# The memory norm's factors in two lots, and the decode output of attention two tiles earlier

## The chip, the cores and the metric

One core of one Trainium2 chip runs one launch of the program. The metric is the device time of the launch in microseconds (us), the median of several runs. The names of the engines: PE is the matrix engine (TensorE), DVE VectorE, ACT ScalarE, POOL GpSimd, SP SyncE, whose work here is to issue DMAs; each takes its instructions in an order fixed when the program is built.

## The reference

One step of a decoder layer over a prompt of 1024 tokens and a sample group of 8 sequences with one new token each. Only the part around the change is given:

```python
xp = xp + merge_groups(oa, o_r, gr, subln_a[l], lam_init).astype(xp.dtype) @ w_out[l]
mk_p, mv_p = mem_kv(mem_prompt, norm_mem_kv[l], w_mk[l], w_mv[l])
xp = xp + mem_attend(rmsnorm(xp, norm_mem_q[l]), mk_p, mv_p, w_mq[l], w_mo[l])
xp = xp + sq_relu_mlp(rmsnorm(xp, norm_mlp[l]), w_up[l], w_down[l])

def rmsnorm(x, g):
    xf = x.astype(jnp.float32)
    y = xf * lax.rsqrt(jnp.mean(xf * xf, axis=-1, keepdims=True) + EPS)
    return (y * g.astype(jnp.float32)).astype(x.dtype)

def mem_attend(h, mk, mv, w_mq, w_mo):
    q = (h @ w_mq).reshape(B, T, H_M, DH_M)
    s = jnp.einsum('bthd,bmhd->bhtm', q, mk.astype(q.dtype)).astype(jnp.float32) * DH_M ** -0.5
    p = jax.nn.softmax(s, axis=-1)
    ...
```

The sample group goes through the same lines with the same weights; its attention reads caches of keys and values by pages. All is float32 and the model width is 1024.

## The kernel before

The 1024 prompt tokens and the 8 decode tokens stand side by side as T = 1032 columns, cut into three thirds of CH = 344; c = 2 is the third (columns 688 to 1031), which holds the decode tokens. Activations lie with the features on the partitions, eight feature tiles of 128. Each operand of a product is split into a high and a low part (UH and UL, wh and wl), so that one product of 8 feature tiles is 24 matmuls.

A weight unit u (512 KB) is loaded by SP into `raw_u`, cast to `wh_u` by ACT and subtracted to `wl_u` by DVE. `raw` has three buffers, `wh` and `wl` four. The query weights of memory attention are u48 to u55, two units for each of four pairs of feature tiles.

`proj_residual` multiplies attention's output by `w_out` and adds the residual. Its tiles `pr_o_ft_c` go in the order (0,0), (0,1), (1,0) ... (7,1), and then the late third (0,2) ... (7,2). The first five of the late third are begun with half of their terms behind (7,1) and finished later, because the decode columns of the other half are not there yet. Behind each tile DVE adds the residual into `x2_ft` (L1447), ACT squares it, and POOL adds the square to `ssum2` (L1497). The finished `x2` is stored to DRAM as X2 (L1587), and it is split with the norm's gain into UH and UL: 688 columns early, the late third at the end.

Beside these tiles the steps of `decode_values` run: attention of the decode tokens over cached values. They sum into `dacc` on DVE; then `dop` (two matmuls) sums over partitions, `oda` (ACT, DVE and POOL) normalises the heads, and `dtr` (four transposes) brings the result into the decode columns of UH and UL. A list of tiles, `when`, says behind which tile a step goes.

`rstd_bcast` makes the norm's factors: matmuls with a vector of ones sum the squares over the features into `rs`; ACT copies the sums into a row; SP moves that row into 86 partitions (`rcol`); DVE and POOL take the power -0.5; SP stores the factors to DRAM (`rrow`, row 2) and reads them back into all partitions as `rb2`. The query product `mq_pr_f_c` does not need the factors; they multiply its result (L1679, into `qm`), for which six PSUM banks are there.

From the decode columns of `qm` POOL makes `qdm`, DVE `dex_m`, and PE `rep_m_0`, a transposed copy of the decode queries, which stands behind the second pair's two late products. In the same stretch the memory's keys and values are prepared: `memT` (split to `mh` and `ml`) and `memn` (squared, `mjk`), whose own factors `rm` are stored to DRAM in single floats (L1629) and read back as `rmb` (L1631).

The code is written in program order, and a scheduler merges it into one order for each engine and for SP's queue. `pin` holds PE's matmuls to the written order.

Of the kernel before, what the change touches and what calls it, by code (L numbers as in the profile page):

```python
# [19 lines left out]
P = 128  # L20
D = 1024
# [27 lines left out]
def decoder_step(ctx: ExitStack, tc: tile.TileContext, i: dict, o: dict):  # L49
# [24 lines left out]
    def mm(out, l, r, start, stop):  # L74
        pinned(nc.tensor.matmul(out, l, r, start=start, stop=stop))  # L75
# [4 lines left out]
    def mm3(out, terms, lo=0, hi=None):  # L80
        n = len(terms)
        for x, (lh, ll, rh, rl) in list(enumerate(terms))[lo:hi]:
            mm(out, lh, rh, x == 0, False)
            mm(out, lh, rl, False, False)
            mm(out, ll, rh, False, x == n - 1)
# [51 lines left out]
    def rsqrt_small(out, ss, n, scale, p=P):  # L137

        nc.vector.tensor_scalar(ss, ss, scale, EPS, ALU.mult, ALU.add)
        nc.gpsimd.tensor_tensor(out, ss, half[:p, 0:1].to_broadcast([p, n]), op=ALU.pow)  # L140
# [28 lines left out]
    def bcast_rows(row_ap, p, n):  # L169
        return bass.AP(tensor=row_ap.tensor, offset=row_ap.offset, ap=[[0, p], [1, n]])  # L170
# [1253 lines left out]
            pass  # L1424


    def proj_residual(A, bank, base, ktorder, xsrc, xdst, ssum, nm, us0, steps, when, parts, ahead=0, early=None, stage=()):

        squares = []
        units = {p: us0[2 * p : 2 * p + 2] for p in range(len(us0) // 2)}

        def fetch(p):
            if p not in units:
                units[p] = [unit(base + 2 * p + x, parts(2 * p + x) if p > 1 else None, nc.gpsimd if p == 1 else None) for x in range(2)]
            for ft in (2 * p, 2 * p + 1):
                nc.sync.dma_start(xdst(ft), xsrc(ft))

        def terms(ft, c):
            return proj_terms(units[ft // 2], ft % 2, c, ktorder)

        def store(ps, ft, c):
            cs = slice(c * CH, c * CH + CH)
            xd = xdst(ft)[:, cs]
            nc.vector.tensor_add(xd, ps[:, :CH], xd)  # L1447
            seen["DVE"] = nc.cur_bb.bb.instructions[-1]
            if (ft, c) == (7, 2):
                last = A.tile([P, WMAX], F32, tag="sqc", name=f"sqc_{nm}_7_2", bufs=2)[:, :CH]  # L1450
                nc.scalar.activation(last, xd, AF.Square)
                squares.append(last)
            else:
                add_squares(A, xd, ssum, cs, ft == 0, f"{nm}_{ft}_{c}")


        order = [(ft, c) for ft in range(8) for c in range(2)] + [(ft, 2) for ft in range(8)]
        fetch(0)
        fetch(1)
        early = early or {}  # L1460
        pin[0] = ahead > 0
        for ft, c in order[:ahead]:
            if (ft, c) not in early:
                early[ft, c] = bank(f"pr_{nm}_{ft}_{c}"), 0
            ps, done = early[ft, c]
            mm3(ps[:, :CH], terms(ft, c), done, 7)
            early[ft, c] = ps, 7
        for ft, c in order:
            if (ft, c) in ((1, 1), (2, 1)):
                fetch(ft + 1)  # L1470
            if (ft, c) in early:
                ps, done = early[ft, c]
                mm3(ps[:, :CH], terms(ft, c), done)
            else:
                pin[0] = False
                ps = bank(f"pr_{nm}_{ft}_{c}")
                mm3(ps[:, :CH], terms(ft, c))
            seen["PE"] = nc.cur_bb.bb.instructions[-1]
            store(ps, ft, c)
            if (ft, c) in when:  # L1480
                next(steps)
            if (ft, c) == (7, 1):
                for some in stage:
                    for x in some:
                        early[x] = bank(f"pr_{nm}_{x[0]}_{x[1]}"), 4
                        mm3(early[x][0][:, :CH], terms(*x), 0, 4)
                    seen["PE"] = nc.cur_bb.bb.instructions[-1]
                    next(steps)
        return squares[0]

    def add_squares(A, x, ssum, cs, first, nm):
        if first:
            nc.scalar.activation(ssum[:, cs], x, AF.Square)
        else:
            sq = A.tile([P, WMAX], F32, tag="sqc", name=f"sqc_{nm}", bufs=2)[:, : cs.stop - cs.start]
            nc.scalar.activation(sq, x, AF.Square)
            nc.gpsimd.tensor_add(ssum[:, cs], ssum[:, cs], sq)  # L1497

    def rstd_bcast(A, PS, bufs, ssum, last, r, dst, nm, rtag):

        row = A.tile([P, T], F32, tag=rtag, name=f"rrow_{nm}")[:1]
        rp = PS.tile([P, 512], F32, tag="acc", name=f"rs_{nm}", bufs=bufs)
        sums = [rp[32 * c : 32 * c + 1, :CH] for c in range(3)]
        for c in range(3):
            mm(sums[c], ones, ssum[:, c * CH : c * CH + CH], True, c < 2)
        mm(sums[2], ones, last, False, True)
        for c in range(3):
            nc.scalar.copy(row[:, c * CH : c * CH + CH], sums[c])
        col = A.tile([86, 12], F32, tag="rcol", name=f"rcol_{nm}")
        nc.sync.dma_start(col, row)  # L1510
        rc = A.tile([86, 12], F32, tag="rrc", name=f"rrc_{nm}")
        rsqrt_small(rc, col, 12, 1.0 / D, 86)
        nc.sync.dma_start(rrow[r : r + 1, :].rearrange("a (p c) -> p (a c)", p=86), rc)
        nc.sync.dma_start(dst, bcast_rows(rrow[r : r + 1, :], P, T))

    with pool("x2") as XP:
        x2 = [XP.tile([P, T], F32, tag=f"x2_{ft}", name=f"x2_{ft}") for ft in range(8)]
# [2 lines left out]
        with pool("c") as A:  # L1520
            def decode_values():
# [26 lines left out]
                with tc.issue_after(seen["PE"]):  # L1548
# [12 lines left out]
                    odv = oda.rearrange("p (h v) -> p h v", h=4)  # L1561
                    nc.vector.tensor_mul(odv, odv, r4.unsqueeze(2).to_broadcast([8, 4, P]))
                yield
                with tc.issue_after(seen["PE"]):
                    tr = dt("dtr")
                    for h in range(4):
                        nc.tensor.transpose(tr[:, h * 8 : h * 8 + 8], oda[:, h * P : h * P + P], ident[:8, :8])
                    odT = tr[:, :32].rearrange("p (k c) -> p k c", k=4)
                    for h in range(4):
                        split_gain(odT[:, h, :], subln8, h, NT, T, gcol=0)  # L1570
                yield


            ssum = A.tile([P, T], F32, tag="ssum", name="ssum2")
            last = proj_residual(
                A, out_bank, U_OUT, OUT_KT, lambda ft: i["xT"][:, ft, :], lambda ft: x2[ft], ssum, "o", us_out, decode_values(),
                [(ft, c) for ft in range(4) for c in range(2)] + [(4, 1)],
                lambda x: [
                    G.tile([P, T], F32R, tag="rb2", name="wlo_3")[:, :1024] if (nm, x) == ("wl", 7)
                    else A.tile([P, 1024], F32R, tag=f"{nm}{x}", name=f"{nm}o_{x}") for nm in ("wh", "wl")  # L1580
                ],
                ahead=len(OUT_EARLY), early=early_out, stage=([(0, 2), (1, 2)], [(2, 2), (3, 2), (4, 2)]),
            )
            rb2 = G.tile([P, T], F32, tag="rb2", name="rb2")
            rstd_bcast(A, PB, 2, ssum, last, 2, rb2, "2", "dacc")
            for ft in range(8):
                nc.sync.dma_start(X2[ft], x2[ft])  # L1587
        bc_ps.close()
# [7 lines left out]
    with pool("d") as A:  # L1596
# [62 lines left out]
        for pr in range(4):  # L1659
            us = [unit(U_MQ + 2 * pr + x) for x in range(2)]  # L1660
            for f in range(2):
                qm.append(A.tile([P, T], F32, tag=f"qm{2 * pr + f}", name=f"qm_{2 * pr + f}"))

            late = [(0, 2), (1, 2)]
            rest = [(0, 0), (0, 1), (1, 0), (1, 1)]
            for f, c in late + rest if pr else rest + late:
                q = qm[2 * pr + f]
                cs = slice(c * CH, c * CH + CH)
                ps = PS.tile([P, 512], F32, tag="acc", name=f"mq_{pr}_{f}_{c}", bufs=6)
                mm3(  # L1670
                    ps[:, :CH],
                    [
                        (us[kt // 4][0][:, (kt % 4) * 256 + f * P : (kt % 4) * 256 + f * P + P],
                         us[kt // 4][1][:, (kt % 4) * 256 + f * P : (kt % 4) * 256 + f * P + P],
                         UH[:, kt, cs], UL[:, kt, cs])
                        for kt in range(8)
                    ],
                )
                nc.vector.scalar_tensor_tensor(q[:, cs], ps[:, :CH], -1.0 / 16.0, rb2[:, cs], ALU.mult, ALU.mult)  # L1679
                if c == 2:  # L1680
                    nc.gpsimd.tensor_copy(qdm[:, 2 * pr + f, :], q[:, NT:])
                if (f, c) == (1, 2) and pr % 2:
                    for _ in dec:
                        pass
                    dec = dec_scores(pr // 2)
                    next(dec)
                for _ in range(3 if pr == 3 else 1):
                    next(dec, None)
# [938 lines left out]
```

## Time and profile before

| | |
|---|---|
| median of 3 runs | 1488.96 us (1487.69 to 1489.63) |
| the profiled execution's own time | 1496.69 us |
| its span, first to last instruction | 1494.8 us |
| mean granted clock of PE | 0.995 |
| PE busy | 1471.7 us, 98% of the span |
| DVE, ACT, POOL busy | 73%, 45%, 21% |
| mean DMA rate | 158 GB/s |

The profile is one execution; times in it are counted from its first instruction, and L with a number is a line of the kernel before. Buffer numbers are left out of the names there, so `pr_o` stands for all its tiles and `rb` for `rb2`. A number behind `<-` in brackets is the idle time of the engine before an instruction, and the name there what ended it.

### The profile page before, as it was taken

The numbers are of one execution on the slowest core, as the hardware profiler recorded it, in microseconds if no ns is written. First come the engines' busy times: TensorE is split into PE (matmuls) and PEld (weight loads), VectorE is DVE, ScalarE is ACT, GpSimd is POOL, SyncE is SP. The second block draws the span as 40 slices with busy tenths as digits, with TensorE's granted clock in tenths as the row PEclk, the third lists the DMA queues.
The fourth block names the chain that finished last, engine by engine and source line by source line (L and its number), as shares of the span: only waits on it lengthen the run. The fifth ranks groups of instructions, "written<-read, shape, count | busy, mean of one in ns | idle before, by whom it ended". The sixth has DMA issues, their size and how long they took to land.

```text
span 1494.8 us, 27880 instructions
## 1 busy us (share of the span) xinstructions
PE 1471.7 (98%) x10925; PEld 1401.8 (94%) x10925; DVE 1098.7 (73%) x2264; ACT 679.6 (45%) x1325; POOL 321.1 (21%) x346
## 2 busy tenths in 40 slices
PE   9999999998999999999999999999999999999997
PEld 7899779998779999989999999999999999999997
DVE  7666436887767636567886988888888879787865
ACT  7543435665552431248535643434334443343454
POOL 0035323123414311105022100000001311110380
PEclk9999999999999999999999999999999999999998
DMA  8255728213847157474582444344436774536273
GB/s 287 65 185 180 202 58 189 71 47 110 268 145 283 59 195 175 145 228 102 178 304 68 136 148 145 128 154 157 156 139 209 239 251 142 171 101 198 72 128 114
DMA packets 125238, 236.69 MB, mean 158 GB/s; under 512 B 13748, under 2 KB 76521, under 8 KB 124978
## 3 DMA queue, kind: packets, MB, share of 16 engines
q1 hardware_dynamic: 89064, 170.51, 36.0%
q0 software_dynamic: 24912, 44.80, 11.0%
q10 hardware_dynamic: 11130, 19.60, 3.5%
q8 instruction: 86, 1.41, 0.4%
q14 instruction: 46, 0.38, 0.1%
HBM read 170.25 MB, written 57.52 MB: 152 GB/s over the span
## 4 chain that ended last, share of the span: by engine, by line
PE 84%; DVE 8%; ACT 3%; issue 2%; DMA 2%; POOL 0%; ACTq 0%; another core or an unknown queue 0%; SPq 0%; DVEq 0%; POOLq 0%
PE dn L2309 19%; PE Z L2143 9%; PE qkp L75 7%; PE mq L75 6%; PE Y L2143 6%; PE X L2143 6%; PE pr_o L75 6%; PE pr_m L75 4%; PE grp L75 3%; PE sp L75 2%; PE av L75 2%; PE mv L75 1%; PE mk L75 1%; PE mpv L75 1%; PE vap_z L522 1%
## 5 line engine op out<-in xcount | busy, mean ns | idle before, releaser
L2309 PE MATMUL dn<-UH,wd 128*128 128x258 f32 x1792 | 325.1, 283 | 0.8 <-DVE c L2413 0.3
L2309 PEld LDWEIGHTS dn<-UH,wd 128*128 128x128 f32 x1792 | 277.6, 189 | 1.8 <-issue 0.8
L2309 PE MATMUL dn<-UL,wd 128*128 128x258 f32 x896 | 252.7, 282 | 0.0
L2309 PEld LDWEIGHTS dn<-UL,wd 128*128 128x128 f32 x896 | 169.0, 189 | 0.0
L2413 DVE TENSOR_TENSOR c<-c,dn 128x258 f32<-128x258 f32 x216 | 88.5, 417 | 38.2 <-PE dn L2309 35.8
L2169 ACT ACTIVATE hq<-r 128x258 f32<-128x258 f32 x128 | 53.9, 422 | 114.1 <-DVE r L2168 114.1
L2143 PE MATMUL X<-UH,wu 128*128 128x258 f32 x512 | 97.4, 282 | 0.9 <-ACT p L2194 0.9
L2143 PE MATMUL Z<-T_h,wu 128*128 128x258 f32 x512 | 98.2, 284 | 0.0
L2287 ACT CAST wd<-raw_d 128x512 fp32r<-128x512 f32 x96 | 58.8, 620 | 78.4 <-PE dn L2309 73.2
L1953 ACT CAST wu<-raw_up 128x512 fp32r<-128x512 f32 x96 | 59.2, 617 | 62.2 <-PE Z L2143 54.7
L2280 ACT CAST UH<-raw_h 128x1032 fp32r<-128x1032 f32 x56 | 58.8, 1057 | 55.0 <-PE dn L2309 27.3
L2143 PEld LDWEIGHTS X<-UH,wu 128*128 128x128 f32 x512 | 81.3, 188 | 1.1 <-ACT p L2194 1.1
L2143 PEld LDWEIGHTS Z<-T_h,wu 128*128 128x128 f32 x512 | 81.3, 189 | 0.0
L2281 DVE TENSOR_TENSOR UL<-raw_h,UH 128x1032 fp32r<-128x1032 f32 x56 | 73.4, 1311 | 9.9 <-ACT UH L2280 9.9
L2180 POOL DMA_DIRECT2D HT<-ht x32 | 17.2, 536 | 292.4 <-DVE ht L2179 291.9
L2288 DVE TENSOR_TENSOR wd<-raw_d,wd 128x512 fp32r<-128x512 f32 x96 | 72.0, 757 | 10.0 <-ACT wd L2287 9.9
L2143 PE MATMUL Z<-T_l,wu 128*128 128x258 f32 x256 | 72.3, 282 | 0.0
L2143 PE MATMUL X<-UL,wu 128*128 128x258 f32 x256 | 72.3, 282 | 0.0
L128 ACT CAST wh_u<-raw_u 128x1024 fp32r<-128x1024 f32 x43 | 44.7, 1049 | 54.2 <-PE mq L75 31.2
L1954 DVE TENSOR_TENSOR wu<-raw_up,wu 128x512 fp32r<-128x512 f32 x96 | 64.5, 684 | 3.7 <-ACT wu L1953 3.7
L129 DVE TENSOR_TENSOR wl_u<-raw_u,wh_u 128x1024 fp32r<-128x1024 f32 x39 | 51.6, 1328 | 18.3 <-ACT wh_u L128 18.1
L2301 POOL TENSOR_TENSOR raw_d<-raw_d,raw_d 128x512 f32<-128x512 f32 x16 | 22.1, 1382 | 194.5 <-DVE raw_d L2297 173.4
(598 smaller groups left out, 4718.2 us busy)
## 6 DMA issues: line engine op xcount, KB each, us to landing
raw_u<-in_wall SPq DMA_DIRECT2D x49, 512.0 KB
HT<-ht POOLq DMA_DIRECT2D x32, 516.0 KB
raw_h<-HT SPq DMA_DIRECT2D x32, 516.0 KB
raw_up<-in_wall SPq DMA_DIRECT2D x32, 512.0 KB
raw_d<-in_wall SPq DMA_DIRECT2D x32, 512.0 KB
HQ<-hq ACTq DMA_DIRECT2D x32, 387.0 KB
raw_h<-HQ SPq DMA_DIRECT2D x24, 516.0 KB
cmk<-in_cmk SPq DMA_DIRECT2D x16, 512.0 KB
```

Of the source, the lines that this page charges most:

```text
L75: pinned(nc.tensor.matmul(out, l, r, start=start, stop=stop))
L129: (lo_engine or nc.vector).tensor_sub(wl[:, :n], raw[:, :n], wh[:, :n].bitcast(F32))
L1953: nc.scalar.copy(w[:, :512], src)
L1954: nc.vector.tensor_sub(w[:, 512:], src, w[:, :512].bitcast(F32))
L2143: pinned(nc.tensor.matmul(ps, l, r[:, k, :], start=first and k == 0 and x == 0, stop=k == 3 and x == 2, skip_group_check=True))
L2169: nc.scalar.activation(h[:, PLACE[quad], :], r, AF.Square)
L2280: nc.scalar.copy(h, rv)
L2281: nc.vector.tensor_sub(l, rv, h.bitcast(F32))
L2287: nc.scalar.copy(w[:, :512], src)
L2288: nc.vector.tensor_sub(w[:, 512:], src, w[:, :512].bitcast(F32))
L2309: pinned(nc.tensor.matmul(ps, l, r[:, k, cq], start=first and k == 0 and x == 0, stop=k == 3 and x == 2, skip_group_check=True))
L2413: nc.vector.tensor_add(y, y, ps)
```

## The change

It has two parts.

The decode output: `dop` and `oda` go behind tile (6,1); `dtr` stays where it was (an empty step stands between).

The factors: the squares of the late third go into a tile of their own, `third` (`ssum3_o`), which takes one of the three `raw` buffers. The sums of the first two thirds of the columns (`rs_2`) are formed behind tile (4,2), and their factors (8 in each of 86 partitions) go the old way into columns 0 to 687 of `rb2`. The late third's sums (`rs_3`, two matmuls) stand behind the first query product, mq_0_0_0, and their factors (4 in each of 86 partitions) go into the rest of `rb2` by DMAs of their own.

```diff
@@ -1424,12 +1424,12 @@
             pass
 
 
-    def proj_residual(A, bank, base, ktorder, xsrc, xdst, ssum, nm, us0, steps, when, parts, ahead=0, early=None, stage=()):
-        squares = []
+    def proj_residual(A, bank, base, ktorder, xsrc, xdst, ssum, nm, us0, steps, when, parts, sums_done, ahead=0, early=None, stage=()):
+        third = []
         units = {p: us0[2 * p : 2 * p + 2] for p in range(len(us0) // 2)}
 
         def fetch(p):
@@ -1446,10 +1446,13 @@
             xd = xdst(ft)[:, cs]
             nc.vector.tensor_add(xd, ps[:, :CH], xd)
             seen["DVE"] = nc.cur_bb.bb.instructions[-1]
-            if (ft, c) == (7, 2):
-                last = A.tile([P, WMAX], F32, tag="sqc", name=f"sqc_{nm}_7_2", bufs=2)[:, :CH]
-                nc.scalar.activation(last, xd, AF.Square)
-                squares.append(last)
+            if c == 2:
+                if ft == 0:
+                    third.append(G.tile([P, T], F32, tag="raw", name=f"ssum3_{nm}", bufs=3))
+                if ft == 7:
+                    nc.scalar.activation(third[0][:, CH : 2 * CH], xd, AF.Square)
+                else:
+                    add_squares(A, xd, third[0], slice(0, CH), ft == 0, f"{nm}_{ft}_{c}")
             else:
                 add_squares(A, xd, ssum, cs, ft == 0, f"{nm}_{ft}_{c}")
 
@@ -1479,6 +1482,8 @@
             store(ps, ft, c)
             if (ft, c) in when:
                 next(steps)
+            if (ft, c) == (4, 2):
+                sums_done()
             if (ft, c) == (7, 1):
                 for some in stage:
                     for x in some:
@@ -1486,7 +1491,7 @@
                         mm3(early[x][0][:, :CH], terms(*x), 0, 4)
                     seen["PE"] = nc.cur_bb.bb.instructions[-1]
                     next(steps)
-        return squares[0]
+        return third[0]
 
     def add_squares(A, x, ssum, cs, first, nm):
         if first:
@@ -1496,22 +1501,21 @@
             nc.scalar.activation(sq, x, AF.Square)
             nc.gpsimd.tensor_add(ssum[:, cs], ssum[:, cs], sq)
 
-    def rstd_bcast(A, PS, bufs, ssum, last, r, dst, nm, rtag):
-        row = A.tile([P, T], F32, tag=rtag, name=f"rrow_{nm}")[:1]
-        rp = PS.tile([P, 512], F32, tag="acc", name=f"rs_{nm}", bufs=bufs)
-        sums = [rp[32 * c : 32 * c + 1, :CH] for c in range(3)]
-        for c in range(3):
-            mm(sums[c], ones, ssum[:, c * CH : c * CH + CH], True, c < 2)
-        mm(sums[2], ones, last, False, True)
-        for c in range(3):
+    def token_rstd(cols, row, sums, terms, r, cs, nm):
+        n = (cs.stop - cs.start) // 86
+        for c in range(n // 4):
+            for x, y in enumerate(terms):
+                mm(sums[c], ones, y[:, c * CH : c * CH + CH], x == 0, x == len(terms) - 1)
+        for c in range(n // 4):
             nc.scalar.copy(row[:, c * CH : c * CH + CH], sums[c])
-        col = A.tile([86, 12], F32, tag="rcol", name=f"rcol_{nm}")
-        nc.sync.dma_start(col, row)
-        rc = A.tile([86, 12], F32, tag="rrc", name=f"rrc_{nm}")
-        rsqrt_small(rc, col, 12, 1.0 / D, 86)
-        nc.sync.dma_start(rrow[r : r + 1, :].rearrange("a (p c) -> p (a c)", p=86), rc)
-        nc.sync.dma_start(dst, bcast_rows(rrow[r : r + 1, :], P, T))
+        col, rc = cols[:, 0:n], cols[:, n : 2 * n]
+        nc.sync.dma_start(col, row[:, : n * 86])
+        rsqrt_small(rc, col, n, 1.0 / D, 86)
+        nc.sync.dma_start(rrow[r : r + 1, cs].rearrange("a (p c) -> p (a c)", p=86), rc)
+    def spread_rstd(dst, r, cs):
+        nc.sync.dma_start(dst[:, cs], bcast_rows(rrow[r : r + 1, cs], P, cs.stop - cs.start))
 
     with pool("x2") as XP:
         x2 = [XP.tile([P, T], F32, tag=f"x2_{ft}", name=f"x2_{ft}") for ft in range(8)]
@@ -1561,6 +1565,7 @@
                     odv = oda.rearrange("p (h v) -> p h v", h=4)
                     nc.vector.tensor_mul(odv, odv, r4.unsqueeze(2).to_broadcast([8, 4, P]))
                 yield
+                yield
                 with tc.issue_after(seen["PE"]):
                     tr = dt("dtr")
                     for h in range(4):
@@ -1572,17 +1577,25 @@
 
 
             ssum = A.tile([P, T], F32, tag="ssum", name="ssum2")
-            last = proj_residual(
+            early_tokens, late_tokens = slice(0, 2 * CH), slice(2 * CH, T)
+            def first_rstd():
+                rp = PB.tile([P, 512], F32, tag="acc", name="rs_2", bufs=2)
+                row = A.tile([P, T], F32, tag="dacc", name="rrow_2")[:1]
+                cols = A.tile([86, 16], F32, tag="rcol", name="rcol_2")
+                token_rstd(cols, row, [rp[32 * c : 32 * c + 1, :CH] for c in range(2)], [ssum], 2, early_tokens, "2")
+            third = proj_residual(
                 A, out_bank, U_OUT, OUT_KT, lambda ft: i["xT"][:, ft, :], lambda ft: x2[ft], ssum, "o", us_out, decode_values(),
-                [(ft, c) for ft in range(4) for c in range(2)] + [(4, 1)],
+                [(ft, c) for ft in range(4) for c in range(2)] + [(4, 1), (6, 1)],
                 lambda x: [
                     G.tile([P, T], F32R, tag="rb2", name="wlo_3")[:, :1024] if (nm, x) == ("wl", 7)
                     else A.tile([P, 1024], F32R, tag=f"{nm}{x}", name=f"{nm}o_{x}") for nm in ("wh", "wl")
                 ],
-                ahead=len(OUT_EARLY), early=early_out, stage=([(0, 2), (1, 2)], [(2, 2), (3, 2), (4, 2)]),
+                first_rstd, ahead=len(OUT_EARLY), early=early_out, stage=([(0, 2), (1, 2)], [(2, 2), (3, 2), (4, 2)]),
             )
             rb2 = G.tile([P, T], F32, tag="rb2", name="rb2")
-            rstd_bcast(A, PB, 2, ssum, last, 2, rb2, "2", "dacc")
+            spread_rstd(rb2, 2, early_tokens)
             for ft in range(8):
                 nc.sync.dma_start(X2[ft], x2[ft])
         bc_ps.close()
@@ -1667,6 +1680,7 @@
                 q = qm[2 * pr + f]
                 cs = slice(c * CH, c * CH + CH)
                 ps = PS.tile([P, 512], F32, tag="acc", name=f"mq_{pr}_{f}_{c}", bufs=6)
+                pin[0] = (pr, f, c) == (0, 0, 0)
                 mm3(
                     ps[:, :CH],
                     [
@@ -1676,6 +1690,12 @@
                         for kt in range(8)
                     ],
                 )
+                if pin[0]:
+                    token_rstd(
+                        third[:86, 2 * CH : 2 * CH + 8], A.tile([P, T], F32, tag="qm7", name="rrow_3")[:1], [dt("rs_3")[:1, :CH]],
+                        [third[:, :CH], third[:, CH : 2 * CH]], 2, late_tokens, "3")
+                    spread_rstd(rb2, 2, late_tokens)
+                    pin[0] = False
                 nc.vector.scalar_tensor_tensor(q[:, cs], ps[:, :CH], -1.0 / 16.0, rb2[:, cs], ALU.mult, ALU.mult)
                 if c == 2:
                     nc.gpsimd.tensor_copy(qdm[:, 2 * pr + f, :], q[:, NT:])
```

In the scheduled orders more moves than these lines. On PE before, all sums stand ahead of the query product (`rs_2` of the three thirds; `sqc_o_7_2` is the last square):

```order
L75 MATMUL pr_o_7_2_5602<-UL_67,who_7_5057 128x344
L75 MATMUL pr_o_7_2_5602<-UH_66,wlo_3_5058 128x344
L75 MATMUL rs_2_5632<-ssum2_4950,ones_62 1x344 x3
L75 MATMUL rs_2_5632<-sqc_o_7_2_5628,ones_62 1x344
L75 MATMUL mq_0_0_0_5757<-UH_66,wh_u48_5745 128x344
L75 MATMUL mq_0_0_0_5757<-UL_67,wh_u48_5745 128x344
```

On PE now, first behind pr_o_4_2 and then behind mq_0_0_0:

```order
L75 MATMUL pr_o_4_2_5440<-UH_66,wlo_5_5010 128x344
L75 MATMUL rs_2_5545<-ssum2_4950,ones_62 1x344 x2
L75 MATMUL pr_o_5_2_5556<-UH_66,who_4_5003 128x344
...
L75 MATMUL mq_0_0_0_5753<-UH_66,wl_u49_5748 128x344
L75 MATMUL rs_3_5779<-ssum3_o_5479,ones_62 1x344 x2
L75 MATMUL mq_0_0_1_5789<-UH_66,wh_u48_5741 128x344
```

The sums went from ahead of the query product to these two places.

SP's queue before, from the factors' row on (`rcol_2`, `rrow` and `rb2` are the norm's factors; `rm` is the store of the memory factors):

```order
L1510 DMA rcol_2_5640<-rrow_2_5631 86x1x12
L1513 DMA rrow_75<-rrc_2_5642 86x12
L1514 DMA rb2_5630<-rrow_75 128x1032
L1606 DMA g_mkv_5699<-in_g_mkv 128x8
L1613 DMA memT_0_5705<-in_memT 128x1024
L1613 DMA memT_1_5715<-in_memT 128x1024
L1624 DMA memn_0_5726<-in_mem 128x1024
L1624 DMA memn_1_5730<-in_mem 128x1024
L1643 DMA cmk_0_0_5997<-in_cmk 128x2x512
L1643 DMA cmk_0_2_6029<-in_cmk 128x2x512
L1629 DMA rrow_75<-rm_5734 128x2x1
L1643 DMA cmk_0_4_6061<-in_cmk 128x2x512
```

SP's queue now, first from the store of X2 to the early factors and then the part with the late ones (`ssum3_o` is now also the place of the late factors' 86 partitions):

```order
L1600 DMA X2_71<-x2_4_4941 128x1032
L1513 DMA rcol_2_5547<-rrow_2_5546 86x1x8
L122 DMA raw_u49_5745<-in_wall 128x1024
L1600 DMA X2_71<-x2_5_4942 128x1032
L1515 DMA rrow_75<-rcol_2_5547 86x8
L122 DMA raw_u50_5921<-in_wall 128x1024
L1600 DMA X2_71<-x2_6_4943 128x1032
L122 DMA raw_u51_5927<-in_wall 128x1024
L1518 DMA rb2_5641<-rrow_75 128x688
L1600 DMA X2_71<-x2_7_4944 128x1032
L122 DMA raw_u52_6131<-in_wall 128x1024
L122 DMA raw_u53_6137<-in_wall 128x1024
```

```order
L1619 DMA g_mkv_5695<-in_g_mkv 128x8
L1626 DMA memT_0_5701<-in_memT 128x1024
L1626 DMA memT_1_5711<-in_memT 128x1024
L1637 DMA memn_0_5722<-in_mem 128x1024
L1513 DMA ssum3_o_5479<-rrow_3_5778 86x1x4
L1637 DMA memn_1_5726<-in_mem 128x1024
L1656 DMA cmk_0_0_6003<-in_cmk 128x2x512
L1515 DMA rrow_75<-ssum3_o_5479 86x4
L1656 DMA cmk_0_2_6035<-in_cmk 128x2x512
L1642 DMA rrow_75<-rm_5730 128x2x1
L1518 DMA rb2_5641<-rrow_75 128x344
L1656 DMA cmk_0_4_6067<-in_cmk 128x2x512
```

The loads of u48 to u52, which stood ahead of all stores of X2 before, now stand among them; u53 and u52 stand ahead of `memT`; the late factors' row, second last of these rows, stands behind the store of `rm`.

ACT before, around the last square of the late third:

```order
L144 ACTIVATE UH_66<-x2_2_4939,g_mq_4945 128x344
L144 ACTIVATE UH_66<-x2_3_4940,g_mq_4945 128x344
L1451 ACTIVATE sqc_o_7_2_5628<-x2_7_4944 128x344
L144 ACTIVATE UH_66<-x2_7_4944,g_mq_4945 128x344
L1508 COPY rrow_2_5631<-rs_2_5632 1x344 x3
```

ACT now, at the same place:

```order
L144 ACTIVATE UH_66<-x2_3_4940,g_mq_4945 128x344
L128 CAST wh_u50_5923<-raw_u50_5921 128x1024
L1453 ACTIVATE ssum3_o_5479<-x2_7_4944 128x344
L144 ACTIVATE UH_66<-x2_7_4944,g_mq_4945 128x344
L128 CAST wh_u51_5929<-raw_u51_5927 128x1024
L1511 COPY rrow_3_5778<-rs_3_5779 1x344
```

The casts of u50 and u51 went in between the late splits and the square.

## The prediction

> **What bounds the kernel now.** I read the busy shares first, then the chain that ended last.
>
> ```profile
> PE 1471.7 (98%) x10925; PEld 1401.8 (94%) x10925; DVE 1098.7 (73%) x2264; ACT 679.6 (45%) x1325; POOL 321.1 (21%) x346
> PE 84%; DVE 8%; ACT 3%; issue 2%; DMA 2%; POOL 0%; ACTq 0%; another core or an unknown queue 0%; SPq 0%; DVEq 0%; POOLq 0%
> ```
>
> PE is the bound from end to end, so a term counts only if it takes PE time away or leaves PE waiting. In the stretch that the change touches (495 to 640 us) the waits of PE are two:
>
> ```profile
> PE dtr L1567 <- DVE oda L1562: 1.0, 1, 1.0
> PE rs L75 <- ACT sqc_o L1451: 1.0, 1, 1.0
> ```
>
> The timeline of PE shows both places (columns: start, duration, instruction, idle before), and the chain that ended last, in order of time, what comes after:
>
> ```profile
> 505.93 1.03 PE L75 MATMUL dop<-dacc,selgt 128*8 128x512 f32 x4
> ...
> 512.50 0.32 PE L75 MATMUL pr_o<-UH,wlo 128*128 128x344 f32 x1
> 513.82 0.38 PE L1567 MATMUL dtr<-ident,oda 8*128 8x8 f32 x4 [1.00 <-DVE oda L1562]
> ...
> 535.02 0.32 PE L75 MATMUL pr_o<-UH,wlo 128*128 128x344 f32 x1
> 535.27 0.75 PE L75 MATMUL rs<-ssum,ones 128*1 128x344 f32 x6
> 537.01 0.74 PE L75 MATMUL rs<-sqc_o,ones 128*1 128x344 f32 x2 [0.98 <-ACT sqc_o L1451]
> 537.68 0.42 PE L75 MATMUL mq<-UH,wh_u 128*128 128x344 f32 x1
> ```
>
> ```profile
> 512.99 0.69 DVE oda L1562
> ...
> 537.75 30.34 PE mq L75 x192
> 568.08 0.22 PE rep_m L854 x2
> ...
> 569.31 0.22 PE rep_m L854
> ```
>
> A matmul of 344 columns takes PE 30.34 / 192 = 0.158 us in the stream.
>
> The sums of squares keep PE from the query product from 535.18 (535.02 + 0.16) to 537.68: 2.5 us, of which 0.98 is waiting. The factors that follow from them bind nothing in this trace: no PE wait follows. All my terms are differences; they are made against this execution's 1494.8 us span (its own time was 1496.69, the median of the runs 1488.96), and I carry them to the median one for one.
>
> **The decode output two tiles earlier.** `dop` moves from behind three half groups to ahead of pr_o_7_0; its two matmuls cost the same there. The sums that it needs are old by then. Everything between `dop` and the transposes took 7.8 us before (505.93 to 512.99 + 0.69) and now has the two tiles and five half groups, 108 matmuls by 0.158 = 17 us. So the wait of 1.0 goes. The `oda` steps now stand on DVE ahead of the sum of pr_o_7_0 and hold it up by a few us; the banks are seven and the next user of that bank is seven groups on, so this costs nothing. Taken: -1.0; bounds -1.1 and -0.8.
>
> **The sums in two lots.** The three first matmuls of `rs` ran side by side in 0.75 (six passes, 535.27). Two of them move behind pr_o_4_2, where `ssum` has long been summed: +0.8 there. The third lot is two matmuls into one row, one after the other: a single one took 537.68-537.01 = 0.67, so 1.3, behind the first query product. Against 2.5 before this is -0.4.
>
> ```profile
> 529.08 0.92 POOL L1497 TENSOR_TENSOR ssum<-ssum,sqc_o 128x344 f32<-128x344 f32 x1 [2.18 <-ACT sqc_o L1496]
> 541.46 2.28 POOL L140 TENSOR_TENSOR rrc<-rcol,half 86x12 f32<-86x12 f32 x1 [7.35 <-DVE rcol L139]
> ...
> 532.94 3.03 ACT L144 ACTIVATE UH<-x,g_mq 128x344 fp32r<-128x344 f32 x6
> 536.46 0.49 ACT L1451 ACTIVATE sqc_o<-x 128x344 f32<-128x344 f32 x1 [0.49 <-DVE x L1447]
> ```
>
> It presumes that the last square is there when PE has done mq_0_0_0, 24 matmuls or 3.8 us after the last pr_o. With both terms the last pr_o ends at 535.0 (535.18-1.0+0.8), so the square is due at 538.8. ACT now casts wh_u50 right ahead of it, and raw_u50 is loaded only behind the first factors on SP's queue: pr_o_5_2 ends 48 matmuls before 535.0, at 527.4; its sum and square (0.5 each), POOL's addition (0.9) and POOL's power (8 columns, so 1.6 of the 2.28 for 12) bring that to 531, and the load to 531.5. A load of that size with nothing in front took 3.6 us (`memn`, below): landed at 535.1. ACT's splits end at 536.0, then the cast (about 1.0) and the square (0.5): 537.5. This hides, with 1.3 us to spare; bounds 0 and +1.5, as far as the stores in front may hold the load.
>
> **The queues that it is moved past.** On SP the loads of u48 to u53 now stand between and behind the X2 stores, and the row of the late factors stands behind `memT` and `memn`. On DVE the subtractions wl_u49 to wl_u51, done by 524.8 before, fall among the last splits:
>
> ```profile
> 523.59 1.23 DVE L129 TENSOR_TENSOR wl_u<-raw_u,wh_u 128x1024 fp32r<-128x1024 f32 x1 [0.41 <-ACT wh_u L128]
> ...
> 535.87 0.50 DVE L1447 TENSOR_TENSOR x<-pr_o,x 128x344 f32<-128x344 f32 x1
> 536.29 1.74 DVE L145 SCALAR_TENSOR_TENSOR UL<-x,g_mq,UH 128x344 fp32r<-128x344 f32 x3
> ```
>
> The splits ended at 538.0; with two and a half such subtractions (1.2 each) wl_u51 ends near 541. raw_u53 waits for it, because it gets raw_u51's buffer, and `g_mkv` and `memT` stand behind it. What follows `memT` then goes as it did, only earlier:
>
> ```profile
> 545.47 0.33 SPq L1514 DMA_DIRECT2D rb<-rrow  x1
> 546.76 0.38 SPq L1613 DMA_DIRECT2D memT<-in_memT  x1
> ...
> 555.40 0.33 SPq L1624 DMA_DIRECT2D memn<-in_mem  x1
> ...
> 561.26 0.37 SPq L1629 DMA_DIRECT2D rrow<-rm  x1
> 561.73 0.41 SPq L1643 DMA_DIRECT2D cmk<-in_cmk  x1
> ...
> 570.47 0.34 SPq L1631 DMA_DIRECT2D rmb<-rrow  x1
> ```
>
> ```profile
> 552.73 3.32 ACT L1617 ACTIVATE mh<-memT,g_mkv 128x256 fp32r<-128x256 f32 x8 [13.61 <-DMA memT<-in_memT]
> 559.04 1.06 ACT L1626 ACTIVATE mjk<-memn 128x1024 f32<-128x1024 f32 x1 [1.94 <-DMA memn<-in_mem]
> ```
>
> `memT` was issued at 546.76; now, as far behind raw_u53 as it stood behind `rb` (1.3), at 542.3, 4.5 us earlier. The second `memn` (issue 555.40, landed by 559.04) gives the memory factors `rm`, whose store was issued at 561.26; now, with two sums of queries less in between, near 556.3. This store decides the case: in the changed order the late `rb2` row (SP's row after `rm`) stands right behind it.
>
> **What stands behind the store of `rm`.** It writes 256 single floats. The wait for it and the next DMA behind it:
>
> ```profile
> SPq L1631 <- DMA rrow<-rm: 8.3, 1, 8.3
> SPq L1245 <- DMA atd<-qblkd: 3.6, 1, 3.6
> ```
>
> ```profile
> 548.98 0.94 DVE L1679 SCALAR_TENSOR_TENSOR qm<-mq,rb 128x344 f32<-128x344 f32 x2 [7.60 <-DMA rb<-rrow]
> 575.02 0.43 DVE L1652 CUSTOM_DVE_ANT_0 cmk<-cmk,qrm 128x256 f32<-128x256 f32 x1 [1.55 <-DMA cmk<-in_cmk]
> ```
>
> The store took from 561.26 to 570.47, 9.2 us; the other store of single floats here (`atd`, 32 of them) also kept SP waiting 3.6. The `cmk` load behind it took from 561.73 to 575.02: 13.3 us, against 3.6 for `memn` with nothing in front. The late row is the same kind of transfer as `rb`, which took 3.5 with nothing in front (545.47 to 548.98), and a third of its size. Issued at 556.7, it lands between 560.2 (unhindered) and 570.0 (like that `cmk`). I take 566.2, just after the store (556.3 + 9.2), since it stands in the same queue and is smaller than `cmk`.
>
> [...]
>
> **Who waits for the late row.** DVE's sums of column 2, then POOL's copies of the decode columns, then the `dex` copies, then PE's `rep_m_0`, which stands eight query groups on (568.08 before):
>
> ```profile
> 560.30 0.51 DVE L1679 SCALAR_TENSOR_TENSOR qm<-mq,rb 128x344 f32<-128x344 f32 x1
> 561.56 1.22 DVE L129 TENSOR_TENSOR wl_u<-raw_u,wh_u 128x1024 fp32r<-128x1024 f32 x1
> 564.76 0.51 DVE L1679 SCALAR_TENSOR_TENSOR qm<-mq,rb 128x344 f32<-128x344 f32 x1
> ```
>
> PE comes to `rep_m_0` at 535.0 + 30.3 + 1.3 = 566.7 and to its last transpose 1.2 later (569.31-568.08). On DVE the way from the first of these sums to the third is 4.5 (560.30 to 564.76); with the fourth (0.4), POOL's copy and two `dex` copies the last operand is there 5.7 after the row lands. So PE waits L + 5.7 - 567.9: nothing if the row lands by 562.2, and 4.0 if at 566.2. Bounds 0 and 7.8. PE has nothing else in its order there, so it is lost.
>
> **The clock after such a wait.** One earlier wait of PE shows it:
>
> ```profile
> 355.68 0.55 PE L78 MATMUL trA<-ident,e 128*128 128x128 f32 x3 [2.04 <-DVE e L1015]
> ```
>
> ```profile
> 356.20:359.60 3.40, 3.40 (x15) 3.40 (x14) 3.00 (x10) 1.41 (x3) 0.00 (x0) 0.50 0.00 0
> 360.00:364.00 4.00, 4.00 (x28) 3.92 (x27) 2.80 (x10) 2.71 (x6) 0.41 (x2) 1.00 0.01 2
> ```
>
> After 2.04 us without work the granted clock (third column from the right) was 0.50 for 3.4 us, and PE did 15 matmuls where at 28 per 4.0 us it would have done 24: 9 by 0.143 = 1.3 us lost. A wait of 4.0 should be: +1.3, bounds 0 and +1.7 (half of 3.4).
>
> [...]
>
> **The sum.** -1.0 - 0.4 + 4.0 + 1.3 = +3.9 us: 1488.96 + 3.9 = 1492.9, or 0.26% slower. What a measurement of this kernel can tell from no change is about 0.2%, 3.0 us: 1486.0 to 1491.9.
>
> **Rivals.**
> - The late row comes in time. It decides by 562.2, that is 5.9 us after the `rm` store is issued, or if that store is issued by 552. For it: that row is a small transfer, and `rb` took 3.5. Against: the 13.3 of `cmk`. Then only the gains remain: 1488.96 - 1.4 = 1487.6, not slower.
> - The row is late but the clock stays up: +2.6, 1491.6. [...]
> - The row is as late as that `cmk`, 570.0: -1.4 + 7.8 + 1.3 = +7.7, 1496.7.
> - The sum does not hide behind the first product, because ACT stands at the cast of wh_u50 till raw_u50 lands: PE waits at rs_3 as it did at rs, up to 1.5 more, with the late row pushed by as much again: +3.9 + 1.5 = +5.4 at most, 1494.4. For it: this load stands behind two DMAs of the first factors and a store; against: 1.3 us to spare.
>
> **How the numbers follow.** Forecast 0.42, in time 0.20, clock stays up 0.20, as late as `cmk` 0.12, wait at rs_3 0.06. Slower by over 0.2% are the forecast but for a small part (0.39), the two last rivals (0.18), and little of the second (0.03, centre 1491.6): 0.60. Faster by over 0.2% would need twice the gains summed here: 0.04, out of the first rival. The rest, 0.36, is within. The range takes in the first rival's centre and the third's: 1487.2 to 1497.0.
>
> **What would show it.** Right: no wait at `dtr`; `rs` without a wait in both places; in the waits of PE a new one, `rep_m` behind `dex_m`, near 566 us, with the sum of column 2 waiting for `rb`; a granted clock of 0.5 for some 3.4 us after it. Wrong: that wait under 2 us, or an issue time of the `rm` store far from 556; a wait at `mq` for wl_u49 or of `rs` for the square, which I cost at nothing.

## The result, and the profile after

The changed kernel takes 1493.47 us (median of 10 runs, 1489.69 to 1495.41) where the kernel before takes 1488.82 (10 runs beside them): ratio 1.0034, 95% interval 1.0026 to 1.0042. It is slower, by 4.65 us at the medians and by 5.1 us (3.9 to 6.3) by the ratio.

The page of the changed kernel, its first line of busy times and its chain, say no more than before: PE is the bound.

```profile
PE 1471.3 (99%) x10925; PEld 1401.9 (94%) x10925; DVE 1095.4 (73%) x2265; ACT 678.1 (45%) x1325; POOL 320.3 (21%) x347
PE 83%; DVE 7%; DMA 4%; ACT 3%; issue 2%; POOL 0%; SPq 0%; DVEq 0%; ACTq 0%; POOLq 0%
```

The spans can't be subtracted: 1494.8 before and 1491.4 after, though the runs go the other way. The executions differ ahead of the change: near 350 us, for one, PE waits 2.47 and 2.04 us and its clock halves in the profile before (0.50 from 356.20 to 359.60), and waits 0.73 us at full clock in the changed kernel's. So I take the stretch between two matmuls that both kernels have, `vrep` (behind tile (4,1), ahead of everything moved) and the first `mk` (the product behind the last query product). Their rows in PE's timeline, of before and then of the changed kernel:

```profile
478.25 1.12 PE L75 MATMUL vrep<-vdec,selg 8*128 8x512 f32 x2
...
629.60 0.28 PE L75 MATMUL mk<-mh,wh_u 128*128 128x256 f32 x1
```

```profile
472.29 1.12 PE L75 MATMUL vrep<-vdec,selg 8*128 8x512 f32 x2
...
627.51 0.28 PE L75 MATMUL mk<-mh,wh_u 128*128 128x256 f32 x1
```

151.35 us before, 155.22 after: +3.87. A second profile of the kernel before gives 151.36 (476.56 to 627.92), so the stretch repeats within 0.01 us while whole executions differ by several microseconds.

In the stretch both old waits of PE are gone, and there is one new one:

```profile
PE rep_m L854 <- DVE dex_m L853: 3.4, 3, 1.7
```

PE's timeline shows the two lots of sums and the place of the wait:

```profile
517.24 0.75 PE L75 MATMUL rs<-ssum,ones 128*1 128x344 f32 x4
...
532.47 0.32 PE L75 MATMUL mq<-UH,wl_u 128*128 128x344 f32 x1
532.72 1.32 PE L75 MATMUL rs<-ssum_o,ones 128*1 128x344 f32 x4
533.97 0.42 PE L75 MATMUL mq<-UH,wh_u 128*128 128x344 f32 x1
...
561.21 0.30 PE L854 MATMUL rep_m<-ident,dex_m 128*128 128x128 f32 x1 [0.60 <-DVE dex_m L853]
563.19 0.33 PE L854 MATMUL rep_m<-ident,dex_m 128*128 128x128 f32 x1 [1.69 <-DVE dex_m L853]
...
565.31 0.43 PE L854 MATMUL rep_m<-ident,dex_m 128*128 128x128 f32 x1 [1.16 <-DVE dex_m L853]
```

Behind that wait stands the late row. SP's queue, DVE's first sum of column 2, and the chain of work at this place:

```profile
550.62 0.37 SPq L1642 DMA_DIRECT2D rrow<-rm  x1
551.50 0.34 SPq L1518 DMA_DIRECT2D rb<-rrow  x1
...
558.63 0.33 SPq L1644 DMA_DIRECT2D rmb<-rrow  x1
```

```profile
560.03 0.52 DVE L1699 SCALAR_TENSOR_TENSOR qm<-mq,rb 128x344 f32<-128x344 f32 x1 [9.86 <-DMA rb<-rrow]
```

```profile
551.50 8.43 DMA rb<-rrow
...
560.03 0.53 DVE qm L1699
...
565.31 0.43 PE rep_m L854
```

The `rm` store, issued at 550.62, is over when `rmb`, which waits for it, is issued at 558.63: 8.0 us. The row behind it lands 8.43 after its issue, at 559.9, 1.3 us behind the store.

The clock, in two windows (length, PE busy with its count, granted clock, DMA share, GB/s):

```profile
562.00:565.40 3.40, 1.05 (x7) 1.00 1.01 314
565.40:568.80 3.40, 3.40 (x13) 0.50 0.57 171
```

PE worked only 1.05 us of the first window, and in the second it was granted half its clock and did 13 matmuls.

### The profile page after: what moved, and what is told of

Read it like the earlier page. It is cut to its first block, busy times and chain, and to the rows that moved or that the text cites. A ratio compares the mean times of both kernels' runs of the same rounds, so it can differ in the third digit from the quotient of the medians.

```text
span 1491.4 us, 27883 instructions
## 1 busy us (share of the span) xinstructions
PE 1471.3 (99%) x10925; PEld 1401.9 (94%) x10925; DVE 1095.4 (73%) x2265; ACT 678.1 (45%) x1325; POOL 320.3 (21%) x347
## 4 chain that ended last, share of the span: by engine, by line
PE 83%; DVE 7%; DMA 4%; ACT 3%; issue 2%; POOL 0%; SPq 0%; DVEq 0%; ACTq 0%; POOLq 0%
PE dn L2329 19%; PE Z L2163 9%; PE qkp L75 7%; PE pr_o L75 6%; PE Y L2163 6%; PE X L2163 6%; PE mq L75 4%; PE pr_m L75 4%; PE grp L75 3%; PE sp L75 2%; PE av L75 2%; PE mv L75 2%; PE mk L75 1%; PE mpv L75 1%; PE vap_z L522 1%
```

## The experiments

Each ratio is to the kernel before, run in turn on the same chip, with its 95% interval. "Stretch" is the time from `vrep` to `mk` in the one profile taken, less the 151.35 of before. A line `...` in a diff stands for lines left out.

| kernel | median us (before) | ratio | stretch us | PE waits at |
|---|---|---|---|---|
| changed | 1493.47 (1488.82) | 1.0034 (1.0026 to 1.0042) | +3.87 | rep_m 3.4 |
| row_first | 1491.54 (1491.82) | 0.9998 (0.9985 to 1.0011) | -1.50 | none |
| cmk_behind | 1496.48 (1491.82) | 1.0035 (1.0022 to 1.0047) | +3.86 | rep_m 3.5 |
| rm_pairs | 1491.63 (1491.82) | 1.0001 (0.9990 to 1.0012) | -0.90 | rep_m 0.5 |
| rm_act | 1494.73 (1491.82) | 1.0027 (1.0014 to 1.0040) | +1.07 | rep_m 2.3 |
| col_first | 1489.42 (1492.21) | 0.9980 (0.9971 to 0.9989) | -1.52 | none |
| rep_later | 1489.50 (1492.21) | 0.9982 (0.9973 to 0.9991) | -1.61 | none |
| dop_only | 1490.44 (1492.21) | 0.9991 (0.9981 to 1.0001) | -1.20 | rs 1.0 |
| col_one | 1491.25 (1492.21) | 0.9992 (0.9983 to 1.0001) | -1.31 | rs 0.7 |
| col_behind2 | 1488.99 (1491.70) | 0.9977 (0.9967 to 0.9987) | -2.07 | none |

### row_first: the store behind the row

```diff
         rsqrt_small(rm, sm2, 2, 1.0 / D)
-        nc.sync.dma_start(rrow[1:2, :256].rearrange("a (t p) -> p (a t)", p=P), rm)
...
                     spread_rstd(rb2, 2, late_tokens)
+                    with tc.issue_after(seen["late"]):   # the row's DMA
+                        nc.sync.dma_start(rrow[1:2, :256].rearrange("a (t p) -> p (a t)", p=P), rm)
```

> The store of rm moves from ahead of the late rb2 row to right behind it in SP's queue; all else keeps its order. Theory A (the row waits behind the store in the queue): the row, issued near 551.5 in the changed kernel's time, lands in about 3.5 us as rb2 did alone, near 555, ahead of the 556.5 from which rep_m_0 waits; no wait of rep_m and no half clock there, 4 to 5 us less than the changed kernel: 0.999 to 1.000 of the kernel before. Rival B (the row is held up by the 1 MB of cmk loads ahead of it): these stand ahead as before, so it lands near 558 to 560 and the time stays at 1.002 to 1.0035.

SP's queue and DVE's first sum of column 2 in its trace:

```profile
554.27 0.33 SPq L1518 DMA_DIRECT2D rb<-rrow  x1
554.65 0.43 SPq L1699 DMA_DIRECT2D rrow<-rm  x1
...
563.68 0.34 SPq L1701 DMA_DIRECT2D rmb<-rrow  x1
```

```profile
559.47 0.52 DVE L1703 SCALAR_TENSOR_TENSOR qm<-mq,rb 128x344 f32<-128x344 f32 x1 [6.34 <-DMA rb<-rrow]
```

The store takes 9.0 us (554.65 to 563.68; in the eight kernels with single floats where it was read, it took from 7.5, in col_behind2, to 9.2, in the kernel before), but now the row no longer stands behind it. The row needs 5.2 us from issue to the sum instead of 8.5, `rep_m` does not wait, and the stretch falls from +3.87 to -1.50. Exchanging two neighbours in one queue takes away the whole loss. (Whether the 1.5 gained in the stretch also shows in the runs, 0.9985 to 1.0011 cannot say.) The row is 1.7 us slower than the 3.5 expected, not enough to make PE wait. Whether the loads in front of it cost it that, as the rival had it, is not shown: in col_behind2, where neither a `cmk` load nor the `rm` store stood in front, the row also took 5.1 us (issued at 548.76, its sum at 553.82).

### cmk_behind: no loads in front

The store stays ahead of the row; the first cmk loads go behind both (`raw_u54` is held back as well, so that it does not slip in between).

```diff
...
-                nc.sync.dma_start(rv, i["cmk"][:, k : k + 2, ch])
+                with tc.issue_after(seen["late"]) if half == 0 and 0 <= k < 6 else nullcontext():
+                    nc.sync.dma_start(rv, i["cmk"][:, k : k + 2, ch])
...
```

> The store of rm stays ahead of the late row; the two cmk loads of 512 KB that stood ahead of both now stand behind the row. Theory A (256 single floats are slow by themselves): the store still takes about 8 us (550.6 to 558.6), the row lands near 560, rep_m waits 3 to 4 us and the clock halves: 1.003. Rival B (the store is slow because the loads are in front of it): the store is over in 3 to 4 us, the row lands near 555, no wait: 0.999 to 1.000.

```profile
555.24 0.39 SPq L1642 DMA_DIRECT2D rrow<-rm  x1
555.72 0.41 SPq L1518 DMA_DIRECT2D rb<-rrow  x1
...
563.51 0.32 SPq L1645 DMA_DIRECT2D rmb<-rrow  x1
```

The store still takes 8.3 us, with no cmk load ahead of it; wait (3.5), half clock (0.50 from 570.30 to 573.70) and stretch (+3.86) are those of the changed kernel to 0.1 us. The `cmk` loads are not why the store is slow.

### rm_pairs: half as many pieces

```diff
-        nc.sync.dma_start(rrow[1:2, :256].rearrange("a (t p) -> p (a t)", p=P), rm)
+        nc.sync.dma_start(rrow[1:2, :256].rearrange("a (p t) -> p (a t)", p=P), rm)
...
```

> The store of rm writes each partition's two floats side by side: 128 pieces of 8 bytes where there were 256 of 4 (the key eviction then reads rmb with a stride). Order as in the changed kernel. Theory A, with the time set by the number of pieces: about half of the 8.0 us, so the row lands near 556 to 557 and rep_m waits 0 to 0.6: 0.999 to 1.0005. Rival B (loads in front): no change, 1.003.

```profile
555.80 0.33 SPq L1642 DMA_DIRECT2D rrow<-rm  x1
556.42 0.33 SPq L1518 DMA_DIRECT2D rb<-rrow  x1
560.13 0.32 SPq L1644 DMA_DIRECT2D rmb<-rrow  x1
```

The same kilobyte in 128 pieces of 8 bytes takes 4.3 us instead of 8.0 in 256 of 4. So here the time went with the pieces and not with the bytes: the 128 that are gone took 3.7 us, 29 ns each. The pieces became longer as they became fewer, and this pair does not part the two. The 29 ns are no rule either: in the kernel before, 86 pieces of 48 bytes (the factors, 543.76 to 545.47) took 1.7 us and 32 single floats (`atd`, 443.45 to 448.52, right behind a larger store) 5.1. `rep_m` waits 0.5, at the upper end of what was expected.

### rm_act: the store in another queue

```diff
-        nc.sync.dma_start(rrow[1:2, :256].rearrange("a (t p) -> p (a t)", p=P), rm)
+        nc.scalar.dma_start(rrow[1:2, :256].rearrange("a (t p) -> p (a t)", p=P), rm)
...
```

> The store of rm is issued by ACT on its own queue instead of SP's; the row keeps its place. Theory A as an order within one queue: the row lands near 555, no wait, 0.999 to 1.000. Rival C (the single floats keep the DMA engines busy for any queue): the row still lands after the store, near 559 to 560, and the time stays at 1.002 to 1.0035.

ACT's queue, SP's queue and DVE:

```profile
553.29 0.39 ACTq L1642 DMA_DIRECT2D rrow<-rm  x1
```

```profile
554.15 0.33 SPq L1518 DMA_DIRECT2D rb<-rrow  x1
...
562.29 0.33 SPq L1700 DMA_DIRECT2D rmb<-rrow  x1
```

```profile
562.08 0.52 DVE L1702 SCALAR_TENSOR_TENSOR qm<-mq,rb 128x344 f32<-128x344 f32 x1 [9.25 <-DMA rb<-rrow]
```

Here rival C was right in the main, and my theory, as an order within SP's queue, too narrow. With the store in another queue the row still takes 7.9 us, against 5.2 in row_first, and lands as the store ends (562.0 and 562.3). While the store was under way in the changed kernel, from 553 to 558, the DMAs moved 10 to 36 GB/s, although the row and a `cmk` load of 512 KB behind it had been issued (551.50 and 551.94). So it is not the order within one queue alone that holds the row up; by what the store in the other queue delays it was not shown. What the other queue gains is about a microsecond of waiting: 2.3 instead of 3.4, and in this profile no half clock (1.00 from 561.70 to 571.90). The runs (0.27% slower) say more than this profile's stretch (+1.07, 0.07%). The profiled execution was the fastest of the twelve (1491.58, the slowest 1500.46); whether the others wait longer or lose the clock was not seen.

### col_first: the whole late chain earlier

The late sums' row goes into its partitions ahead of `memT` and `memn`.

```diff
+        seen["col"] = ...                            # the DMA of the late sums' row
...
+                with tc.issue_after(seen["col"]):
                     nc.sync.dma_start(raw[:, :1024], i["memT"][:, 4 * x : 4 * x + 4, :])
```

> The late sums' row is moved into its partitions (the first DMA of the late factors) ahead of memT and memn instead of behind them; the late rb2 row then stands some 5 us ahead of the rm store. Theory A (all of the loss comes from the row behind the store): no wait of rep_m, the gains of dtr (1.0) and of the sums (0.4) remain: about 1.5 us under the kernel before in the touched stretch, ratio 0.998 to 1.000. Rival: memT, held back by that one DMA, makes another step late (the memory factors, the cmk loads), and a wait of 1 us or more shows up behind rep_m: 1.000 to 1.002.

```profile
538.83 0.64 SPq L1513 DMA_DIRECT2D ssum_o<-rrow  x1
539.64 0.82 SPq L1633 DMA_DIRECT2D memT<-in_memT  x2
...
546.47 0.33 SPq L1519 DMA_DIRECT2D rb<-rrow  x1
555.20 0.38 SPq L1647 DMA_DIRECT2D rrow<-rm  x1
```

The row is issued 8.7 us ahead of the store, which is as slow as before (8.6 us, 555.20 to 563.84) and in nobody's way. No wait of PE is left in the stretch, and by the ratios (0.9980 here, 1.0034 for the changed kernel) it is faster than both, the one before and the changed one.

### rep_later: the wait covered instead

```diff
-                if (f, c) == (1, 2) and pr % 2:
+                if (f, c) == ((0, 1) if pr == 1 else (1, 2)) and pr % 2:
```

> The changed kernel with rep_m_0 two query groups later in PE's order (48 matmuls, 7.5 us). The row is as late as before. Theory A (the loss is PE standing at rep_m_0): no wait, no half clock there, 1.4 less than the kernel before in the stretch, ratio 0.998 to 1.000. Rival D (the decode scores of memory are short of time too): the cmk work behind rep_m_0 starts 4 us later than in the changed kernel, the second half's rep_m or a later step waits, and 2 us or more of the loss stay: 1.001 to 1.003.

The row is as late as in the changed kernel (DVE waits 9.66 us for it), but PE has 48 more matmuls to do before `rep_m_0` and does not wait: -1.61. Rival D's later wait did not come: the decode scores have that time to spare.

### dop_only: the first part alone

The kernel before, with `(6, 1)` added to `when` and the empty step.

> The kernel before with the decode output moved up two tiles, and the norm's factors as they were. Theory A: the wait of 1.0 at dtr goes and nothing else moves: 1.0 less in the touched stretch, ratio 0.9985 to 1.0000. Rival: the oda steps on DVE ahead of the sum of pr_o_7_0 make PE wait for a bank: 0.5 us or more back.

The wait at `dtr` is gone and the one at `rs` stays. The stretch is 1.20 shorter, 0.2 more than that wait, and where the 0.2 comes from is open; the interval of the runs reaches to no change.

### col_one and col_behind2: one matmul for the late sums

Both start from col_first and let POOL add the last square too; col_behind2 also puts `rs_3` behind the second query product.

```diff
-                if ft == 7:
-                    nc.scalar.activation(third[0][:, CH : 2 * CH], xd, AF.Square)
-                else:
-                    add_squares(A, xd, third[0], slice(0, CH), ft == 0, f"{nm}_{ft}_{c}")
+                add_squares(A, xd, third[0], slice(0, CH), ft == 0, f"{nm}_{ft}_{c}")
```

> As col_first, and POOL adds the last square into the late third's sums, so that rs_3 is one matmul instead of two. Theory A: another 0.65 less (1.3 to 0.67), about 2.1 us under the kernel before in the touched stretch, ratio 0.9975 to 0.9995. Rival: rs_3 now waits for POOL's addition (0.9 us behind the square), which ends about when PE has done mq_0_0_0: a wait of up to 0.8 at rs_3 and nothing gained over col_first.

> As col_one, with rs_3 (one matmul, POOL's addition of the last square ahead of it) behind the second query product instead of the first, 3.8 us later. Theory A: col_one's wait of 0.7 for POOL goes; the late row, which came some 9 us before it was needed in col_first, comes 4 us later and still costs nothing: 2.1 us under the kernel before from the output tiles to the end of the query product, ratio 0.997 to 0.999. Rival: memT, which stands behind the late sums' row on SP, comes 3 to 4 us later and PE waits behind it, or rep_m waits again: 0.999 to 1.001.

PE's row of the late sums in col_one, then in col_behind2:

```profile
538.54 0.74 PE L75 MATMUL rs<-ssum_o,ones 128*1 128x344 f32 x2 [0.70 <-POOL ssum_o L1499]
```

```profile
539.34 0.74 PE L75 MATMUL rs<-ssum_o,ones 128*1 128x344 f32 x2
```

In col_one the rival was right: PE waits 0.70 for POOL and loses what the second matmul had cost, and the interval of its runs reaches to no change. One product later POOL is done: -2.07 where 2.1 was expected, and the fastest kernel of the study, 0.23% under the kernel before.

### before_again: the kernel before once more

> The kernel before once more, for a second profile: from the output tiles to the end of the query product it should take the same time as in its first profile within 0.1 us, with the two waits of 1.0 (dtr, rs), since the spread between executions should lie outside this stretch. Rival: the stretch itself varies by 0.5 us or more, and the sums made from single profiles are worth less.

151.36 against 151.35, with the same two waits of 1.0. For this stretch a single profile is enough, as far as two profiles of one kernel tell; where a wait may or may not cost the clock, as in rm_act, it says less.

## Why the prediction was right, step by step

In the changed kernel's trace `vrep` comes 5.96 us earlier than in the trace on which the prediction was made, all of it from ahead of the change. Times of the prediction are given less 5.96.

- **dtr, -1.0.** Right: the wait is gone, and alone it gives -1.20.
- **The sums, -0.4.** Right: the lots cost 0.75 (517.24) and 1.34 (from 532.47 + 0.16 to 533.97), 2.1 together, where there were 2.5. The last square was done at 531.5, 1.2 ahead of PE, so wh_u50's cast hid as the margin of 1.3 said; the fourth rival did not come.
- **The queues.** The `rm` store was forecast for 550.3 and issued at 550.62, the row for 550.7 and 551.50. `memT` was forecast for 536.3 and issued at 535.90. The row right behind the store, as forecast, was what decided (row_first).
- **The landing.** Forecast 560.2, measured 559.9. The guess that the row lands just after the store was better than either bound (554.2 and 564.0, the third rival's). The reason given for it, the same queue, was too narrow: in rm_act the row waits with the store in another queue. The store itself took 8.0 us for one kilobyte where 9.2 were forecast, and 4.3 for the same bytes in half the pieces (rm_pairs).
- **The wait, +4.0.** Measured 3.4. With the landing of 559.9 the forecast's own formula gives 3.7; the rest is the way from the row to PE's last operand, which took 5.4 (559.93 to 565.31) where 5.7 was put.
- **The clock, +1.3.** Mis-sized: about 1.8, what is left of +3.87 with -1.0, -0.4 and +3.4. The half-clock window held 13 matmuls where a full one held 24 (rm_act, below), 11 by 0.157 = 1.7. I had scaled from an earlier stretch with other matmuls. The errors of wait and clock cancel, which is luck: together they were forecast at 5.3 and are 5.3.
- **The rival "the clock stays up"** was wrong: the wait came in three pieces, none longer than 1.7, and the clock dropped to 0.50 behind them. That it would drop was no certainty: behind the 2.3 of rm_act it stayed at 1.00 (see the last section).

The stretch says +3.87 and the forecast +3.9. The runs say +4.65 at the medians, with an interval from 3.9 to 6.3 by the ratio. Where the difference lies is open. Besides the place near 350 us the profiles differ near 785 us, where half the clock is granted for one window, with PE busy all through it, in the changed kernel and not in col_first:

```profile
783.80:787.20 3.40, 3.40 (x18) 0.51 0.00 0
```

```profile
780.00:783.40 3.40, 3.40 (x31) 1.00 0.11 39
```

The first profile of the kernel before has that window too (0.50 from 786.29 to 789.70). What sets col_first apart is told in the last section; one profile of each does not tell whether the change makes the window more frequent.

## What to carry to other kernels

Before splitting a small chain of DMAs in two, look at what will stand directly ahead of each piece: a store of 256 single floats took 8 us, and whether the urgent row stood right behind it or right ahead of it decided, in the stretch around it, between 3.9 us lost and 1.5 gained (in the runs between 0.34% lost and no change). Moving such a store to another queue helped little here (0.27% lost instead of 0.34%); issuing it behind what is urgent helped (row_first), and so did half as many pieces of twice the length (rm_pairs, 4.3 us instead of 8.0). And where executions differ by more than the effect, compare a stretch between two instructions that both kernels have, after a second profile of the same kernel has shown that the stretch repeats.

## What was not expected of the hardware

The drops of the clock lie on a raster. In the traces of the kernel before and of the changed one each drop lasts 3.41 us (but the one at the end, which lasts to the last instruction), and within one trace their starts lie whole multiples of 3.413 us apart: 565.40 and 783.85 in the changed kernel, 64 of them; 356.21 and 786.29 before, 126; and in both another 205 to the drop at the end (1483.58 and 1486.02). A step of that raster is called a raster window here. Behind a wait of PE, in the places shown, the clock dropped when PE had been busy less than about half of the raster window just over, whatever the pieces: a drop followed 1.36 us of 3.41 in the kernel before and 1.05 in the changed one, and none followed 2.44 and 2.10 in rm_act, where a wait of 2.3 fell across a boundary. Of before and of rm_act:

```profile
352.80:356.20 3.40, 1.36 (x10) 1.00 0.00 0
356.20:359.60 3.40, 3.40 (x15) 0.50 0.00 0
```

```profile
561.70:565.10 3.40, 2.44 (x16) 1.00 0.67 73
565.10:568.50 3.40, 2.10 (x12) 1.00 1.03 302
568.50:571.90 3.40, 3.40 (x24) 1.00 0.64 210
```

At the waits near 350 us and at `rep_m`, in the five windows read that a drop followed (before, changed, row_first, col_first, cmk_behind), PE was busy for 0.95 to 1.43 us; where the wait left 1.66 (before, 345.97 to 349.38) or more, none came. The kernel before shows both in one trace: its wait of 2.47 us, across the boundary at 349.38, left the clock at 1.00, and its wait of 2.04, inside one window, was followed by 0.50. So a wait of 2 us may or may not cost the clock, as these traces have it by where it falls in the raster; where it did, the estimates are 1.3 us (before) and 1.8 (changed, behind 3.4).

PE's busy time as the profile counts it isn't the whole measure. In the window ahead of the drop near 785 us (780.44 to 783.85 in the changed kernel) PE is busy for 3.15 us, but 16 of its matmuls there, 1.9 us of that, are `opm`, of 8 columns each. Of the changed kernel and of col_first:

```profile
781.11 0.51 PE L75 MATMUL opm<-selgt,daccm 128*128 128x8 f32 x4
782.46 1.40 PE L75 MATMUL opm<-selgt,daccm 128*128 128x8 f32 x12
```

```profile
778.82 0.51 PE L75 MATMUL opm<-selgt,daccm 128*128 128x8 f32 x4
780.18 1.40 PE L75 MATMUL opm<-selgt,daccm 128*128 128x8 f32 x12
```

The kernel before has these sixteen in one raster window as well (783.24 to 785.99, in 782.88 to 786.29, PE busy for 3.15 us), and the drop behind it. In col_first a boundary (779.95, counted from its drop at 349.9) parts them 4 and 12, and the clock stays at 1.00. So in these three profiles what decides there too seems to be where the work falls in the raster, with such short matmuls counting for little. The drop at the end of the program agrees: it follows windows in which 2.47 us (changed) and 2.61 (before) count as busy, 1.24 us of each in matmuls of 1 column. No run moves these matmuls, so this is read from the traces and not shown by an experiment, and the exact measure stays open.
